# Another order for the seven block products of an MLP down-projection, and its b12 loads issued from GpSimd

## The chip, the cores and the metric

The kernel runs on one core of a Trainium2 chip. The metric is device microseconds of one execution; before the change the median of three runs is 2301.19 us (2300.75 to 2302.45). Engines are named as the profile names them: PE (TensorE), DVE (VectorE), ACT (ScalarE), POOL (GpSimd), SP (SyncE, which here only issues DMAs).

## The reference, cut to what matters

Two layers over 256 tokens of width 2048, each a mixer (HGRN2, then gated linear attention) and an MLP, every sub-layer between two RMSNorms and added to the residual. The change lies in the MLP:

```python
def sqrelu_mlp(h, w_up, w_down):
    u = jax.nn.relu(h @ w_up)        # 256 x 2048 by 2048 x 8192
    return (u * u) @ w_down          # 256 x 8192 by 8192 x 2048
...
f = sqrelu_mlp(rmsnorm(h, norm_mlp_pre[i]), mlp_w_up[i], mlp_w_down[i])
h = h + rmsnorm(f, norm_mlp_post[i])
```

All is float32. The kernel multiplies in fp32r with each operand split in a rounded high part and the rest (hi and lo), and adds three products: hi by hi, hi by lo, lo by hi.

## The kernel before, in words

**Splitting.** Weights arrive as "raw" tiles of 128 x 2048 (1 MB) from SP's queue (line 107, three buffers). Each half of a tile is split: ACT writes hi (line 113, `split_hi`), DVE writes lo = raw - hi (line 117, `split_lo`). There are five buffers of hi halves and five of lo halves.

**Groups.** The hidden width of 8192 is worked in eight groups g of 1024. `up(g)` makes the group's activations in eight up products (`gemmT`, lines 165 and 168: 16 matmuls of 512 columns and 16 of 256), and after each pair it combines them into `as` tiles (lines 534 to 542): differences of activations between the two token halves and the two halves of the group, named R, S, S5 and S3.

**Seven products.** The down-projection of a group uses the trick of seven block products in place of eight, on a two by two scheme: two token halves t, two halves h of the group, and a pair of column blocks n0, n1 (512 columns each). Write b11, b21 for the weight blocks of h = 0 and 1 with n0, b12, b22 with n1. The generator `seven(g, p, following)` gives one product at each step (12 matmuls, line 643, split in two halves). Its tiles:

- `run` (pool `sum`, one buffer): first b11 + b12, summed on DVE (line 655); then b22 is added, then b21, each by one accumulating DMA of 1 MB from POOL (`add_to`, line 601).
- `q` (tiles accA and accB, one buffer each): b12, loaded by `load_b12` (line 608) for the following iterator once the present one has split its own q; b22 is added to it by two accumulating DMAs of 512 KB.

The products before, in order: b11 product (bank a), c product (b21, bank c), **first run product** (S by `run`, bank b), S3 product (b22, bank b), **second run product** (S5 by `run`, bank a), q product (R by q, bank a), **third run product** (pure activations by `run`, bank a). The accumulating DMA between two run products can be issued only when both halves of `run` are split for the one, and the splitting for the other can start only when it has landed.

**Full groups.** With p = 0 the columns n0, n1 are blocks 0 and 1, with p = 1 blocks 2 and 3. Groups 1, 3 and 5 (`both`) use `seven` twice; they are the three full groups, in each of the two MLPs. The other groups do blocks 2 and 3 by plain products (`plain`, lines 145 to 147).

**Order.** The loop over g makes group g's eight up products, and between them does steps of group g - 1 by the table `plan`: entry k of it is done after the k-th up product. `a` and `b` are steps of the two iterators, `late` the last step of a full group's second iterator, which falls in the next group's loop. Tile's scheduler then orders each engine's instructions by its own estimate of the time; each engine runs its list strictly in order. So a PE matmul that waits holds all that is behind it.

Of the kernel before, what the change touches and what calls it, by code (L numbers as in the profile page):

```python
# [30 lines left out]
def trunk(  # L31
# [5 lines left out]
    nc = tc.nc  # L37
# [36 lines left out]
    def nm(s):  # L74
        uid[0] += 1
        return f"{s}_{uid[0]}"
# [26 lines left out]
    def load_chunk(wap, idx):  # L103
        if idx in ahead and ahead[idx][0] is wap:
            return ahead.pop(idx)[1]
        raw = wraw.tile([P, 2, 1024], F32, tag="raw", name=nm("raw"))
        nc.sync.dma_start(raw, wap[idx].rearrange("p (k n) -> p k n", k=2))
        return raw
# [10 lines left out]
    def split(raw, into=None):  # L119

        half = split_hi(raw, into)
        split_lo(raw, half)
        return half
# [382 lines left out]
    def mlp(layer, w_up, w_dn, X, rs, ps0, then=None):  # L506
# [22 lines left out]
        R, S, S5, S3 = range(4)  # L529
# [51 lines left out]
        def up(g):  # L581

            for i in range(HK):
                u = tok().rearrange("p (a n) -> p a n", a=2)
                unfold(gemmT(w_up, g * GK + i, X), u[:, 0, :])
                yield
                if i == 0:
                    uT[g] = Xhl(GK)
                    sa[g] = sums_of_a(g)
                unfold(gemmT(w_up, g * GK + HK + i, X), u[:, 1, :])  # L590
                relu_squared(g, u, [i, HK + i])
                yield
                b = u.rearrange("p a (t n) -> p (a t) n", t=NT)
                combine(sa[g][i], b[:, 0, :], b[:, 2, :], b[:, 1, :], b[:, 3, :], b[:, 1:3, :])

        def block(g, h, n):

            return w_dn[n * 16 + 2 * g + h].rearrange("p (k n) -> p k n", k=2)

        def add_to(raw, b):  # L600
            nc.gpsimd.dma_start(raw, b, accum_op=ALU.add)  # L601

        b12 = []

        def load_b12(g, p):
            b12.append([accp.tile([P, 1024], F32, tag=tag, name=nm("bs")) for tag in ("accA", "accB")])
            for j in range(2):
                nc.sync.dma_start(b12[-1][j], block(g, 0, 2 * p + 1)[:, j, :])

        def put(n, t, ps, sign=1):  # L610
            if (n, t) not in m:
                m[n, t] = tok()
                V.tensor_scalar(m[n, t], ps, float(sign), None, ALU.mult)
            else:
                V.tensor_tensor(m[n, t], m[n, t], ps, ALU.add if sign > 0 else ALU.subtract)

        def seven(g, p, following):


            U, n0, n1 = uT[g], 2 * p, 2 * p + 1  # L620
            bank = {}

            def pure(t, h):
                return lambda k: U(HK * h + k, t)

            def summed(c):
                return lambda k: (sa[g][k][:, 0, c, :], sa[g][k][:, 1, c, :])

            def raw_of(h, n):
                raw = load_chunk(w_dn, n * 16 + 2 * g + h)  # L630
                return [raw[:, j, :] for j in range(2)]

            def product(b, x, raw, n, t, sign=1):
                first = b not in bank
                if first:
                    pool, tag = (pstr, "tr") if b == "c" else (pssc, "sc")
                    bank[b] = pool.tile([P, NB], F32, tag=tag, name=nm(f"s{b}"))
                for j in range(2):
                    hi, lo = (w.rearrange("p (k n) -> p k n", k=2) for w in split(raw[j]))
                    for kk in range(2):  # L640
                        xh, xl = x(2 * j + kk)
                        for i, (l, r) in enumerate(((xh, hi), (xh, lo), (xl, hi))):
                            PE.matmul(bank[b], l, r[:, kk, :], start=first and j + kk + i == 0,  # L643
                                      stop=j + kk + i == 4, skip_group_check=not first)
                put(n, t, bank[b], sign)

            b11 = raw_of(0, n0)
            product("a", pure(1, 0), b11, n0, 1)
            yield
            product("c", pure(1, 1), raw_of(1, n0), n0, 1)  # L650
            yield
            tile_ = sump.tile([P, 2, 1024], F32, tag="run", name=nm("bs"))
            run, q = [tile_[:, j, :] for j in range(2)], b12.pop(0)
            for j in range(2):
                V.tensor_tensor(run[j], b11[j], q[j], ALU.add)
            for j in range(2):
                add_to(q[j], block(g, 1, n1)[:, j, :])
            product("b", summed(S), run, n1, 0, -1)
            add_to(tile_, block(g, 1, n1))
            yield  # L660
            product("b", summed(S3), raw_of(1, n1), n1, 1, -1)
            yield
            product("a", summed(S5), run, n1, 1, -1)
            add_to(tile_, block(g, 1, n0))
            yield
            product("a", summed(R), q, n1, 0, -1)
            if following is not None:
                load_b12(*following)
            yield
            product("a", pure(0, 1), run, n0, 0)  # L670
            yield
# [3 lines left out]
        def plain(g, n):  # L675

            ps = [psmm.tile([P, NB], F32, tag="mm", name=nm("mm")) for _ in range(NT)]
            for c in range(2):
                for j, half in enumerate(split_chunk(w_dn, n * 16 + 2 * g + c)):
                    for t in range(NT):  # L680
                        mm_half(ps[t], half, 2 * c + j, uT[g], t, GK)
                if c:
                    for t in range(NT):
                        put(n, t, ps[t])
                yield
# [6 lines left out]
        for i, (g, p) in enumerate(order):  # L692
            it[g, p] = seven(g, p, order[i + 1] if i + 1 < len(order) else None)

        def step(*what):

            for w in what:
                next(w)
# [3 lines left out]
        first = up_first()  # L702
        next(first)
        load_b12(0, 0)
        for _ in first:
            pass
        for g in range(1, NG):
            u = up(g)
            a = it[g - 1, 0]
            late = [it[g - 2, 1]] if g - 2 in both else []  # L710
            n2, n3 = (plain(g - 1, n) for n in (2, 3))
            if g - 1 in both:
                b = it[g - 1, 1]
                plan = [[*late, a, a], [a, a], [a], [a], [a, b, b], [b, b], [b], [b]]
            elif g < LAST:
                plan = [[*late, a, a], [a, n2], [a, n2], [a], [n3, a], [n3], [a], []]
            else:
                plan = [[*late, a, a], [a], [a], [a], [a], [a], [], []]
            for what in plan:
                next(u)  # L720
                step(*what)
            next(u, None)
        new_residue()
        nc.sync.dma_start(residue[-1], spill)
        a = it[LAST, 0]
        step(n2, a, a, a, n2, a, n3, a, n3, a)
        g = LAST
        n2 = plain(g, 2)
        for t, n in ((0, 1), (1, 0), (1, 1)):
            post.take(m[n, t], n, t)  # L730
        if ahead is not None:
            ahead.split(2)
# [350 lines left out]

    st = hgrn((2, w_up0, 0, ((w_up0, 4, 2), (w_up0, 5, 1))))
    st = mlp(0, w_up0, w_dn0, *st, then=(1, w_gin, 16, ((w_gr, 0, 2), (w_gin, 20, 1))))
    st = gla(*st, then=(3, w_up1, 0, ((w_up1, 4, 2), (w_up1, 5, 1))))
    mlp(1, w_up1, w_dn1, *st)


# [70 lines left out]
```

## Time and profile before

| | |
|---|---|
| median of three runs | 2301.19 us |
| the profiled execution | 2299.35 us, its span 2297.5 us |
| PE busy | 98% of the span |
| DVE, ACT busy | 78%, 59% |
| POOL, accumulating loads (line 601) | 88, median 8.5 us to landing |
| SP, b12 loads (line 608) | 44 of 512 KB, median 7.6 us to landing |
| HBM | 222 GB/s over the span |

In the profile a group of instructions is named by line, engine, operation and out<-in; buffer numbers are left out. The up products write `mmT`, the block products `sa`, `sb`, `sc` (banks a, b, c); `sa<-hi,as` is a product with combined activations, `sa<-hi,xhl` one with pure ones. The tiles `run` and `q` both have the name `bs`. A wait in square brackets is idle time of the engine just before that instruction, with what ended it. PE's matmuls overlap in the records; the distance of their starts is what one costs. The granted clock is that of PE, 1.00 at full speed.

### The profile page before, as it was taken

To read this page: it belongs to the slowest core of one execution; us is meant where nothing else is said; L and a number is where in the kernel's file an instruction comes from. 1 tells how busy PE (TensorE), PEld (TensorE's weight loads), DVE (VectorE), ACT (ScalarE), POOL (GpSimd) and SP (SyncE) were. 2 spreads that over 40 slices of the span, in tenths; PEclk is the share of its full clock that TensorE was granted. 3 is DMA by queue.
4 is the path that set the end of the run, shared out by engine and by line. 5 is a ranking of instruction groups with operands and counts; after the bars stand their busy time and mean duration, and the time that the engine had idled before them with its cause. 6 is when DMAs were issued, how large, how long until landed. Compare 5 with 4: busy or idle time off the path is not lost.

```text
span 2297.5 us, 30042 instructions
## 1 busy us (share of the span) xinstructions
PE 2258.2 (98%) x11456; PEld 1919.0 (84%) x11456; DVE 1797.2 (78%) x2505; ACT 1357.4 (59%) x1843; POOL 76.5 (3%) x92
## 2 busy tenths in 40 slices
PE   9999999999999999999999999999999999999998
PEld 7888888888887887887878887888888788888887
DVE  6887877667788788788886767666778878878887
ACT  7554554556565565566667457555656556556564
POOL 0000000000000000000000000000000000000000
PEclk9999999999999999999999999999999999999999
DMA  9544545557788788778964544455778878878895
GB/s 325 170 165 163 184 151 183 189 214 237 235 254 261 227 248 267 218 244 272 284 237 142 207 157 156 165 206 183 248 232 243 271 237 242 272 231 246 273 290 173
DMA packets 82576, 511.23 MB, mean 223 GB/s; under 512 B 9824, under 2 KB 10208, under 8 KB 28800
## 3 DMA queue, kind: packets, MB, share of 16 engines
q1 hardware_dynamic: 69616, 439.84, 52.0%
q0 software_dynamic: 12672, 69.21, 16.5%
q8 instruction: 90, 1.47, 0.2%
q14 instruction: 54, 0.44, 0.1%
q10 hardware_dynamic: 144, 0.26, 0.0%
HBM read 502.99 MB, written 6.29 MB: 222 GB/s over the span
## 4 chain that ended last, share of the span: by engine, by line
PE 86%; DVE 6%; DMA 5%; issue 1%; ACT 1%; SPq 0%; DVEq 0%; ACTq 0%; POOLq 0%
PE mmT L165 23%; PE mmT L168 13%; PE mm L145 11%; PE mm L147 11%; PE mm L146 11%; PE sa L643 8%; PE sb L643 4%; DMA bs<-w_dn 4%; DVE lo L117 3%; PE sc L643 2%; PE sc L804 2%; DMA raw<-w_dn 1%; PE tr L201 1%; DVE xhl L214 1%; ACT hi L113 1%
## 5 line engine op out<-in xcount | busy, mean ns | idle before, releaser
L117 DVE TENSOR_TENSOR lo<-raw,hi 128x1024 fp32r<-128x1024 f32 x732 | 883.6, 1221 | 264.9 <-ACT hi L113 168.6
L113 ACT ACTIVATE hi<-raw 128x1024 fp32r<-128x1024 f32 x732 | 769.2, 1059 | 511.7 <-PE mm L147 203.2
L165 PE MATMUL mmT<-xhl,hi 128*128 128x512 f32 x2704 | 656.2, 391 | 0.0
L165 PEld LDWEIGHTS mmT<-xhl,hi 128*128 128x128 f32 x2704 | 502.3, 188 | 102.1 <-issue 1.4
L146 PE MATMUL mm<-lo,xhl 128*128 128x512 f32 (+1 forms) x1088 | 423.8, 390 | 2.6 <-DVE lo L283 1.2
L145 PE MATMUL mm<-hi,xhl 128*128 128x512 f32 (+1 forms) x1088 | 421.4, 391 | 1.8 <-ACT hi L282 1.2
L147 PE MATMUL mm<-hi,xhl 128*128 128x512 f32 (+1 forms) x1088 | 422.7, 389 | 0.0
L168 PEld LDWEIGHTS mmT<-xhl,lo 128*128 128x128 f32 x2704 | 351.6, 191 | 15.2 <-issue 0.5
L168 PE MATMUL mmT<-xhl,lo 128*128 128x256 f32 x2704 | 358.3, 283 | 0.0
L113 ACT ACTIVATE hi<-bs 128x1024 fp32r<-128x1024 f32 x176 | 185.1, 1059 | 168.0 <-DMA bs<-w_dn 92.1
L117 DVE TENSOR_TENSOR lo<-bs,hi 128x1024 fp32r<-128x1024 f32 x176 | 213.3, 1221 | 80.1 <-ACT hi L113 77.7
L146 PEld LDWEIGHTS mm<-lo,xhl 128*128 128x128 f32 x1088 | 204.5, 188 | 45.1 <-DVE lo L283 2.7
L145 PEld LDWEIGHTS mm<-hi,xhl 128*128 128x128 f32 x1088 | 204.5, 188 | 44.4 <-ACT hi L282 2.8
L147 PEld LDWEIGHTS mm<-hi,xhl 128*128 128x128 f32 x1088 | 204.4, 188 | 42.0 <-issue 0.6
L601 POOL DMA_DIRECT2D bs<-w_dn x88 | 76.3, 875 | 2174.6 <-DVE lo L117 574.1
L643 PE MATMUL sa<-hi,as 128*128 128x512 f32 x352 | 117.5, 395 | 22.2 <-ACT hi L113 22.2
L643 PE MATMUL sb<-hi,as 128*128 128x512 f32 x352 | 121.2, 406 | 0.0
L643 PE MATMUL sa<-hi,xhl 128*128 128x512 f32 x352 | 114.3, 390 | 0.0
L643 PEld LDWEIGHTS sa<-hi,as 128*128 128x128 f32 x352 | 66.4, 189 | 36.3 <-ACT hi L113 23.8
L643 PEld LDWEIGHTS sb<-hi,as 128*128 128x128 f32 x352 | 69.9, 198 | 14.3
L643 PEld LDWEIGHTS sa<-hi,xhl 128*128 128x128 f32 x352 | 66.2, 188 | 13.2
L643 PE MATMUL sb<-lo,as 128*128 128x512 f32 x176 | 71.7, 407 | 0.0
(210 smaller groups left out, 2013.8 us busy)
## 6 DMA issues: line engine op xcount, KB each, us to landing
raw<-w_up SPq DMA_DIRECT2D x128, 1024.0 KB, 6.7
raw<-w_dn SPq DMA_DIRECT2D x106, 1024.0 KB, 7.0
raw<-w_hin SPq DMA_DIRECT2D x56, 1024.0 KB, 4.9
raw<-w_gin SPq DMA_DIRECT2D x48, 1024.0 KB, 4.9
bs<-w_dn POOLq DMA_DIRECT2D x44, 1024.0 KB, 8.8
bs<-w_dn SPq DMA_DIRECT2D x44, 512.0 KB, 7.6
bs<-w_dn POOLq DMA_DIRECT2D x44, 512.0 KB, 7.3
raw<-w_hout SPq DMA_DIRECT2D x16, 1024.0 KB, 4.9
```

Source lines behind the costliest of these rows:

```text
L113: A.activation(hi, raw, AF.Copy)
L117: V.tensor_tensor(half[1], raw, half[0].bitcast(F32), ALU.subtract)
L145: PE.matmul(ps, xh, hi[:, kk, cs], start=(k == 0), stop=False)
L146: PE.matmul(ps, xh, lo[:, kk, cs], start=False, stop=False)
L147: PE.matmul(ps, xl, hi[:, kk, cs], start=False, stop=(k == nk - 1))
L165: PE.matmul(ps, hi, X.both(k), start=(k == 0), stop=False)
L168: PE.matmul(ps[:, 0, :], lo, X.both(k)[:, 0, :], start=False, stop=(k == KT - 1))
L201: PE.transpose(ps[:, j, :], src(j), ident)
L214: V.scalar_tensor_tensor(lo[:, j, :], ps[:, j, :], gain(j), hi[:, j, :].bitcast(F32), ALU.mult, ALU.subtract)
L601: nc.gpsimd.dma_start(raw, b, accum_op=ALU.add)
L643: PE.matmul(bank[b], l, r[:, kk, :], start=first and j + kk + i == 0, stop=j + kk + i == 4, skip_group_check=not first)
L804: PE.matmul(ps[:, hd, :], l(hd * kt + k), r(hd * kt + k), start=(k == 0), stop=(k == kt - 1))
```

## The change

In `seven` the first run product goes to the front, the b11 and c products follow it, and the second run product comes ahead of the S3 product: first run, b11, c, second run, S3, q, third run. `plan` shares the steps out evenly: in a full group two at a time after the up products 1, 2, 3, then one, then two at a time for the second iterator; entry 0 holds only `late`. The plans of the other groups and the steps after the last group follow. The b12 loads go from SP's queue to POOL's. The order in which three finished blocks are normed at the end of an MLP is swapped for two of them.

```diff
         def load_b12(g, p):
             b12.append([accp.tile([P, 1024], F32, tag=tag, name=nm("bs")) for tag in ("accA", "accB")])
             for j in range(2):
-                nc.sync.dma_start(b12[-1][j], block(g, 0, 2 * p + 1)[:, j, :])
+                nc.gpsimd.dma_start(b12[-1][j], block(g, 0, 2 * p + 1)[:, j, :])
...
             b11 = raw_of(0, n0)
-            product("a", pure(1, 0), b11, n0, 1)
-            yield
-            product("c", pure(1, 1), raw_of(1, n0), n0, 1)
-            yield
             tile_ = sump.tile([P, 2, 1024], F32, tag="run", name=nm("bs"))
...
             product("b", summed(S), run, n1, 0, -1)
             add_to(tile_, block(g, 1, n1))
             yield
-            product("b", summed(S3), raw_of(1, n1), n1, 1, -1)
+            product("a", pure(1, 0), b11, n0, 1)
+            yield
+            product("c", pure(1, 1), raw_of(1, n0), n0, 1)
             yield
             product("a", summed(S5), run, n1, 1, -1)
             add_to(tile_, block(g, 1, n0))
+            yield
+            product("b", summed(S3), raw_of(1, n1), n1, 1, -1)
             yield
             product("a", summed(R), q, n1, 0, -1)
...
             if g - 1 in both:
                 b = it[g - 1, 1]
-                plan = [[*late, a, a], [a, a], [a], [a], [a, b, b], [b, b], [b], [b]]
+                plan = [late, [a, a], [a, a], [a, a], [a], [b, b], [b, b], [b, b]]
             elif g < LAST:
-                plan = [[*late, a, a], [a, n2], [a, n2], [a], [n3, a], [n3], [a], []]
+                plan = [late, [a, a], [a, n2], [n2, a], [a, a], [a, n3], [n3], []]
             else:
-                plan = [[*late, a, a], [a], [a], [a], [a], [a], [], []]
+                plan = [late, [a, a], [a], [a], [a], [a], [a], []]
...
-        step(n2, a, a, a, n2, a, n3, a, n3, a)
+        step(n2, a, a, n2, a, n3, a, n3, a, a)
...
-        for t, n in ((0, 1), (1, 0), (1, 1)):
+        for n, t in ((0, 1), (1, 0), (1, 1)):
             post.take(m[n, t], n, t)
```

The scheduler's lists show it at three places. First ACT in the second iterator of group 1 of the first MLP, from the second half of the first run product to the first half of the second one (`bs_1052` and `bs_1041` are the `run` tile). Before:

```order
L113 ACTIVATE hi_1056_6126<-bs_1052_6110 128x1024
L541 ACTIVATE as_787_4635<-tok_1020_5938 128x512
L113 ACTIVATE hi_1059_6140<-raw_1058_6138 128x1024
L113 ACTIVATE hi_1061_6150<-raw_1058_6138 128x1024
L113 ACTIVATE hi_1067_6171<-raw_1066_6169 128x1024
L557 COPY half_1051_6103<-mmT_1045_6060 128x256
L113 ACTIVATE hi_1069_6175<-raw_1066_6169 128x1024
L113 ACTIVATE hi_1072_6214<-bs_1052_6110 128x1024
```

And with the change:

```order
L113 ACTIVATE hi_1045_6080<-bs_1041_6064 128x1024
L113 ACTIVATE hi_1048_6093<-raw_1040_6062 128x1024
L541 ACTIVATE as_787_4635<-tok_1020_5938 128x512
L113 ACTIVATE hi_1050_6103<-raw_1040_6062 128x1024
L113 ACTIVATE hi_1056_6124<-raw_1055_6122 128x1024
L557 COPY half_1039_6055<-mmT_1033_6012 128x256
L113 ACTIVATE hi_1058_6128<-raw_1055_6122 128x1024
L113 ACTIVATE hi_1063_6170<-raw_1061_6167 128x1024
L113 ACTIVATE hi_1065_6180<-raw_1061_6167 128x1024
L551 ACTIVATE xhl_963_5638<-tok_1021_5944 128x2x256
L552 ACTIVATE tok_1021_5944<-tok_1021_5944 128x512
L113 ACTIVATE hi_1067_6191<-bs_1041_6064 128x1024
```

Between the two run products stood the halves of the S3 product and of one up product; now the halves of the b11 product, of one up product and of the c product stand there.

Second, DVE where `run` is summed for that iterator (line 655 before, 651 with the change). Before:

```order
L655 TENSOR_TENSOR bs_1052_6110<-raw_1033_6012,bs_1018_5934 128x1024
L655 TENSOR_TENSOR bs_1052_6110<-raw_1033_6012,bs_1019_5935 128x1024
L553 TENSOR_TENSOR xhl_975_5686<-tok_995_5794,xhl_975_5686 128x2x256
L534 TENSOR_TENSOR tok_1020_5938<-tok_995_5794 128x256
L117 TENSOR_TENSOR lo_1038_6026<-raw_1033_6012,hi_1037_6025 128x1024
```

With the change:

```order
L651 TENSOR_TENSOR bs_1041_6064<-raw_1040_6062,bs_1018_5934 128x1024
L117 TENSOR_TENSOR lo_1036_6016<-raw_1034_6013,hi_1035_6015 128x1024
L651 TENSOR_TENSOR bs_1041_6064<-raw_1040_6062,bs_1019_5935 128x1024
L539 SCALAR_TENSOR_TENSOR tok_1020_5938<-tok_1020_5938,tok_984_5747 128x128
L117 TENSOR_TENSOR lo_1038_6020<-raw_1034_6013,hi_1037_6019 128x1024
L117 TENSOR_TENSOR lo_1044_6071<-bs_1041_6064,hi_1043_6070 128x1024
```

Before, the splits of the b11 product, of the c product and of an up product lay between the sums and the split of `run`; now the split of `run` follows behind the split of one up product.

Third, POOL from the adds into one `run` tile to those into the next, with the change:

```order
L601 DMA bs_972_5691<-w_dn0 128x2048 x2
L608 DMA bs_1018_5934<-w_dn0 128x1024
L608 DMA bs_1019_5935<-w_dn0 128x1024
L601 DMA bs_1018_5934<-w_dn0 128x1024
L601 DMA bs_1019_5935<-w_dn0 128x1024
L601 DMA bs_1041_6064<-w_dn0 128x2048 x2
```

The two rows of line 608 stood in SP's list before, among the raw loads; POOL's list was the same without them.

## The prediction

> **What bounds the kernel now.** I read the page first: the busy shares (part 1) and the chain of waits (part 4).
>
> ```profile
> PE 2258.2 (98%) x11456; PEld 1919.0 (84%) x11456; DVE 1797.2 (78%) x2505; ACT 1357.4 (59%) x1843; POOL 76.5 (3%) x92
> ...
> PE 86%; DVE 6%; DMA 5%; issue 1%; ACT 1%; SPq 0%; DVEq 0%; ACTq 0%; POOLq 0%
> ```
>
> TensorE sets the time, and there is little to win off it: what PE itself loses is the budget. The table of waits says where it loses.
>
> ```profile
> PE sa L643 <- ACT hi L113: 22.2, 7, 4.5
> ...
> ACT hi L113 <- DMA bs<-w_dn: 92.1, 23, 7.8
> ...
> ACT hi L113 <- DMA raw<-w_dn: 61.1, 29, 3.5
> ...
> SPq L608 <- DVE lo L117: 52.5, 32, 2.8
> ```
>
> PE has one large wait: 22.2 us in seven pieces before a block product that goes to bank "a". It waits there for the rounding of a `bs` tile on ScalarE, and ScalarE waits for the DMA into that tile. Raw weight loads also hold ScalarE (61.1 us), but no row of PE names them: the work queued ahead covers them. Next, the timeline at the first of the long pieces (DVE, POOL, ACT and PE, each asked for by itself).
>
> ```profile
> 683.89 2.35 DVE L117 TENSOR_TENSOR lo<-bs,hi 128x1024 fp32r<-128x1024 f32 x2
> ```
> ```profile
> 675.96 0.86 POOL L601 DMA_DIRECT2D bs<-w_dn  x1 [0.27 <-issue]
> 686.54 0.86 POOL L601 DMA_DIRECT2D bs<-w_dn  x1 [9.72 <-DVE lo L117]
> ```
> ```profile
> 698.59 2.00 ACT L113 ACTIVATE hi<-bs 128x1024 fp32r<-128x1024 f32 x2 [6.77 <-DMA bs<-w_dn]
> ```
> ```profile
> 688.75 0.40 PE L643 MATMUL sb<-hi,as 128*128 128x512 f32 x1
> ...
> 691.50 3.79 PE L165 MATMUL mmT<-xhl,hi 128*128 128x512 f32 x16
> 695.13 1.11 PE L168 MATMUL mmT<-xhl,lo 128*128 128x256 f32 x8
> 699.70 0.50 PE L643 MATMUL sa<-hi,as 128*128 128x512 f32 x1 [3.46 <-ACT hi L113]
> ```
>
> This is the second iterator (p = 1) of a full group. DVE ends the split of `run` for the first run product at 686.2; GpSimd then issues the accumulating DMA into `run` (686.54); its data is there at 698.59, 12.05 us later; ScalarE rounds it in 1.1 us; PE starts the second run product at 699.70. PE had reached that matmul at about 696.1 (695.13 and eight 256-wide matmuls): the room for the DMA was 696.1 - 1.1 - 686.54 = 8.5 us. Last the windows, one for each full group's loop, and one loop without a full group.
>
> ```profile
> 630.80:716.40 85.60, 82.14 (x416) 70.11 (x416) 71.12 (x89) 52.46 (x63) 5.17 (x6) 0.98 0.81 247
> 716.40:804.20 87.80, 87.80 (x449) 75.21 (x448) 72.99 (x90) 51.06 (x59) 5.17 (x6) 1.00 0.80 249
> 804.20:891.10 86.90, 82.93 (x415) 70.50 (x414) 71.75 (x91) 52.57 (x64) 5.17 (x6) 0.96 0.81 249
> 978.90:1065.70 86.80, 82.34 (x416) 70.25 (x415) 71.42 (x90) 52.54 (x63) 5.20 (x6) 0.98 0.80 245
> 1730.00:1813.70 83.70, 80.41 (x416) 68.86 (x415) 69.47 (x87) 50.48 (x61) 5.17 (x6) 1.00 0.81 248
> 1901.80:1987.80 86.00, 82.02 (x415) 70.00 (x415) 70.51 (x89) 52.19 (x63) 5.17 (x6) 0.98 0.81 247
> 2075.60:2160.70 85.10, 82.04 (x416) 70.02 (x415) 71.52 (x90) 52.70 (x63) 5.20 (x6) 0.98 0.82 251
> ```
>
> The columns are the stretch, its length, busy time of PE, weight loads, DVE, ACT and POOL, the granted clock, the DMA share and GB/s. All six loops of a full group lose time, the other loop none. They also lose clock: times the lengths, the shares missing from 1.00 are 1.7 + 3.5 + 1.7 + 0 + 1.7 + 1.7 = 10.3 us. What a loop should take comes from these rows of PE:
>
> ```profile
> 589.54 0.40 PE L643 MATMUL sa<-hi,as 128*128 128x512 f32 x1
> ...
> 592.29 3.79 PE L165 MATMUL mmT<-xhl,hi 128*128 128x512 f32 x16
> 595.91 2.08 PE L168 MATMUL mmT<-xhl,lo 128*128 128x256 f32 x16
> 597.83 0.40 PE L145 MATMUL mm<-hi,xhl 128*128 128x512 f32 x1
> ```
>
> A block product takes 592.29 - 589.54 = 2.75 us, an up product 597.83 - 592.29 = 5.54. A full loop has 8 up and 13 block products: 44.3 + 35.8 = 80.1 us. The six loops last 514.1 us against 480.4: 33.7 us too long, which 22.2 (wait) + 10.3 (clock) = **32.5 us** explains to 1.2 us.
>
> **The change, part by part.** Instruction counts and arithmetic stay; PE's work is the same. *First: the run products move apart.* In the full groups' second iterator, the ones that wait now, the first run product is now followed by the b11 product, an up product and the c product before the second: start to start 2.75 + 2.75 + 5.54 + 2.75 = 13.8 us, where before PE came to it after 696.1 - 688.75 = 7.3. The DMA was issued 2.2 us before the first run product started; with that lead the room becomes 13.8 + 2.2 - 1.1 = 14.9 us, with a lead of 1 us (the sum is now formed right ahead of its split) 13.7. Landings:
>
> ```profile
> DMA to landing us min/median/max: 5.5/8.5/11.9
> ```
> ```profile
> DMA to landing us min/median/max: 4.4/7.6/9.3
> ```
> ```profile
> bs<-w_dn SPq DMA_DIRECT2D x44, 512.0 KB, 7.6
> bs<-w_dn POOLq DMA_DIRECT2D x44, 512.0 KB, 7.3
> ```
>
> The first line is of L601, the accumulating loads; the second of L608, the b12 loads. 13.7 is above the longest, 11.9, so the wait goes: -22.2. One thing speaks for a remainder: the two adds into `q` are now issued some 5 us ahead of this one instead of 686.54 - 675.96 = 10.6, and of their 7.3 us about 2.3 are then still to move. 11.9 + 2.3 = 14.2 against 13.7: between 0 and 0.5 us in each of six loops, 0 to 3.0; I take 1.5.
>
> *The clock.* Without the long waits I take all 10.3 us back, since the loop without a wait has 1.00. How long a wait may be without costing clock the rows leave uncertain:
>
> ```profile
> 1798.64 0.50 PE L643 MATMUL sa<-hi,as 128*128 128x512 f32 x1 [3.29 <-ACT hi L113]
> ```
> ```profile
> 2144.03 0.50 PE L643 MATMUL sa<-hi,as 128*128 128x512 f32 x1 [3.06 <-ACT hi L113]
> ```
>
> 3.29 us cost nothing (its loop has 1.00), 3.06 cost 1.7. [...]
>
> *The third run product.* Second to third run product was 16.6 us in the waiting iterator (run, up, q, up, as the plan has it); it is now run, S3, q, up = 13.8. The same 13.7 to 14.9 against 11.9: 0.
>
> *The b12 loads on GpSimd's queue.* They are freed by the split of `q` and are needed by the sum of the next iterator, now its first step. From q product to that first run product lie q, up, third run product, up = 16.6 us of PE. The load is issued about as the q product starts; 11.9 us is the longest landing on that queue; the sum and one rounding follow:
>
> ```profile
> L655 DVE TENSOR_TENSOR bs<-raw,bs 128x1024 f32<-128x1024 f32 x44 | 51.8, 1220 | 11.7 <-DMA raw<-w_dn 11.7
> ```
>
> 11.9 + 2 x 1.22 + 1.06 (as 2.00 for two above) = 15.4 in 16.6: hidden, by 1.2 us at worst. If that cover were gone, 2.4 us at a start. On GpSimd nothing urgent stands behind the load: the next DMA is the add into the same tile. SP loses the 52.5 us it stood at L608; as PE never waits for raw loads, 0. [...]
>
> *The first run product needs the group's combined activations at once.* Before, two pure products covered them. From the copy of an up product's result to the end of the combination:
>
> ```profile
> 589.74 0.37 ACT L557 COPY half<-mmT 128x256 f32<-128x256 f32 x1 [0.85 <-PE mmT L168]
> ```
> ```profile
> 599.40 0.68 DVE L542 TENSOR_TENSOR as<-tok,as 128x512 fp32r<-128x512 f32 x1
> ```
>
> 10.5 us after the up product ended. Cover now: two up products (11.1), and nine matmuls until the last quarter is used (2.0), 13.1: hidden, 2.6 us spare. If it were not, up to 10.5 - 5.5 = 5 us in each of 16 groups.
>
> Sum: -22.2 - 10.3 + 1.5 = -31.0 on the profiled span: 2297.5 - 31.0 = 2266.5. That execution lasted 2299.35 us, 1.85 more than its span and 1.84 below the median of the runs: 2301.19 - 31.0 = **2270 us**.
>
> **The rivals.** (1) *The DMA stays late, less so.* The full loops already have a DMA share of 0.81; without the waits the same bytes go into 80 us, 0.81 x 85.6 / 80.1 = 0.87. If that stretches landings by a quarter (11.9 to 14.9) and the q adds add 2.3, PE waits 17.2 - 14.9 to 17.2 - 13.7, some 2.3 to 3.5 us: at 2.3, without clock loss, 13.8 us over six loops, 2301.2 - 32.5 + 13.8 = 2282. For it: the 12.05 us landing fell in such a crowd. Against: b11 is now held shorter, and fewer loads crowd around it.
> (2) *The change doesn't do what it says.* The scheduler set PE's order, and had put the second run product ahead of the S3 product in the loop above; if it hoists it again, or the same wait turns up at the third, nothing is won: 2299 to 2303. Against: the built order has the c product ahead of it.
> (3) *Slower: DVE at the start of each iterator.* Up, first run and b11 product are 11.0 us of PE. Of DVE's 71 us in a full loop, 42 splits of 1.14 (2.35 for two at 683.89) are 47.9 and four sums 4.9; the rest, 18.2, is 0.87 for each of the 21 products. Here that makes six splits 6.8, two sums 2.4 and three times 0.87, 11.8 us. The five buffers for split halves are a lead (a half feeds 1.4 us of PE in a block product, 2.8 in an up product), in which 0.8 us should drown. If DVE has no lead there, the sums are paid in full at all 22 starts: 51.8 us (the row of L655), 2301.2 - 32.5 + 51.8 = 2320; it decides from 1.5 us a start (32.5 / 22). For it: DVE is 71 us busy in a full loop that is to take 80. Against: in the present trace the sums stand in the same stream, and PE shows no wait on DVE there.
>
> **How the numbers follow.** A measurement of this kernel tells 0.2%, 4.6 us, from no change. Chances: forecast 0.66 (2265 to 2277), (1) 0.19 (2277 to 2293), (2) 0.05, (3) 0.10. Faster 0.85, same 0.05, slower 0.10. The floor is all 33.7 us and a little, 2265; the range reaches through most of (1): 2264 to 2289.
>
> **What would show it.** In the changed profile the PE row on bank "a" waiting for ScalarE should be gone or below 3 us in sum; full loops should last 80 to 81 us at 1.00; DMA share there 0.85 or more. Wrong if a new PE wait on DVE's `lo` or on `hi<-bs` appears at a first run product, if the sum (now L651) shows waits for `bs` loads, or if the half-clock stretches stay without waits.

## The result, and the profile after

The changed kernel takes 2266.78 us, the median of four runs (2266.16 to 2267.66). The kernel before takes 2301.82 us in the same comparison (four runs, 2300.75 to 2303.19). The ratio is 0.9848, with a 95% interval of 0.9831 to 0.9865: the change makes the kernel 1.5% faster. The profiled execution lasted 2267.66 us, its span 2265.9 us.

First the page of the changed kernel, the busy shares and the chain of waits by engine:

```profile
PE 2247.6 (99%) x11456; PEld 1913.6 (84%) x11456; DVE 1798.9 (79%) x2505; ACT 1365.5 (60%) x1843; POOL 101.1 (4%) x136
...
PE 94%; DVE 3%; DMA 1%; ACT 1%; issue 0%; SPq 0%; DVEq 0%; ACTq 0%
```

PE's share of the chain went from 86% to 94%, and DVE's and DMA's shrank from 6% and 5% to 3% and 1%. POOL's 44 more instructions are the b12 loads. The tables of waits of the changed kernel, PE's longest row and then ScalarE's rows on transfers in the MLP (us in total, times, longest):

```profile
PE tr L201 <- DVE h L354: 3.3, 5, 0.9
```
```profile
ACT hi L113 <- DMA raw<-w_dn: 17.7, 9, 3.5
ACT hi L113 <- DMA bs<-w_dn: 11.9, 6, 2.8
ACT hi L113 <- DMA raw<-w_up: 11.4, 9, 2.9
```

The row of 22.2 us on bank a is gone; PE's longest row now has nothing to do with the block products. ScalarE waited 92.1 us for `bs` tiles before, 11.9 us now, and 61.1 and 17.7 us for raw down weights. Landings of the accumulating loads (line 601), where the longest was 11.9:

```profile
DMA to landing us min/median/max: 5.5/8.5/12.5
```

They are much as before. Now the windows of the six full loops, each from the first up product of the group behind a full group to that of the next group (13 block products in each):

```profile
630.80:711.10 80.30, 80.30 (x416) 69.02 (x416) 72.41 (x91) 53.51 (x64) 7.39 (x10) 1.00 0.92 273
798.90:879.20 80.30, 80.30 (x416) 69.01 (x416) 72.16 (x91) 53.16 (x64) 7.41 (x10) 1.00 0.90 268
966.80:1047.20 80.40, 80.40 (x417) 69.11 (x416) 72.56 (x91) 53.41 (x64) 7.39 (x10) 1.00 0.93 273
1710.30:1790.70 80.40, 80.40 (x417) 69.11 (x416) 72.38 (x91) 53.41 (x64) 7.39 (x10) 1.00 0.92 273
1878.30:1958.70 80.40, 80.40 (x418) 69.08 (x417) 72.26 (x91) 53.22 (x64) 7.38 (x10) 1.00 0.92 273
2046.20:2126.60 80.40, 80.40 (x417) 69.10 (x416) 72.26 (x91) 53.16 (x64) 7.38 (x10) 1.00 0.90 266
```

PE is busy over the whole length of each, at full clock. The six last 482.2 us together, where they lasted 514.1 us: 31.9 us less, as much as the span lost (2297.5 - 2265.9 = 31.6). So the whole gain is in the full groups. The transfers are denser than before: the share of the DMA engines is 0.90 to 0.93 where it was 0.80 to 0.82.

The same place as in the prediction, the second iterator of the first full group, in the timeline (POOL, ACT and PE in turn):

```profile
673.88 0.89 POOL L601 DMA_DIRECT2D bs<-w_dn  x1 [8.38 <-DVE bs L651]
676.14 0.88 POOL L601 DMA_DIRECT2D bs<-w_dn  x1 [1.38 <-DVE tok L539]
680.28 0.86 POOL L601 DMA_DIRECT2D bs<-w_dn  x1 [3.26 <-DVE lo L117]
```
```profile
691.40 2.01 ACT L113 ACTIVATE hi<-bs 128x1024 fp32r<-128x1024 f32 x2 [1.42 <-DMA bs<-w_dn]
```
```profile
683.42 0.40 PE L643 MATMUL sb<-hi,as 128*128 128x512 f32 x1
...
697.18 0.39 PE L643 MATMUL sa<-hi,as 128*128 128x512 f32 x1
```

The first two rows are the adds into `q`, the third is the add into `run`, issued 3.1 us before the first run product starts. ScalarE gets its data 11.1 us later. PE comes to the second run product at 697.18 and finds the first half rounded since 692.5: 4.7 us to spare, where it was 3.5 us short.

### The profile page after: what moved, and what is told of

Same layout as the page of the kernel before. It is cut to its first block, busy times and chain, and to the rows that moved or that the text cites. A ratio compares the mean times of both kernels' runs of the same rounds, so it can differ in the third digit from the quotient of the medians.

```text
span 2265.9 us, 30032 instructions
## 1 busy us (share of the span) xinstructions
PE 2247.6 (99%) x11456; PEld 1913.6 (84%) x11456; DVE 1798.9 (79%) x2505; ACT 1365.5 (60%) x1843; POOL 101.1 (4%) x136
## 4 chain that ended last, share of the span: by engine, by line
PE 94%; DVE 3%; DMA 1%; ACT 1%; issue 0%; SPq 0%; DVEq 0%; ACTq 0%
PE mmT L165 27%; PE mmT L168 14%; PE mm L145 10%; PE mm L146 10%; PE mm L147 10%; PE sa L643 10%; PE sb L643 5%; PE sc L643 3%; PE sc L804 2%; DMA wp<-npost 1%; DVE lo L117 1%; DVE xhl L214 1%; PE tr L201 1%; DVE h L354 0%; PE sd L839 0%
## 5 line engine op out<-in xcount | busy, mean ns | idle before, releaser
L168 PE MATMUL mmT<-xhl,lo 128*128 128x256 f32 x2704 | 353.5, 283 | 0.0
L601 POOL DMA_DIRECT2D bs<-w_dn x88 | 76.6, 871 | 926.1 <-DVE lo L117 391.3
L557 ACT COPY half<-mmT 128x256 f32<-128x256 f32 x120 | 44.4, 370 | 72.0 <-PE mmT L168 71.8
L643 PEld LDWEIGHTS sa<-hi,xhl 128*128 128x128 f32 x352 | 66.2, 188 | 13.4
L608 POOL DMA_DIRECT2D bs<-w_dn x44 | 24.3, 553 | 1187.5 <-PE mm L147 974.4
```

The source lines that it names most:

```text
L168: PE.matmul(ps[:, 0, :], lo, X.both(k)[:, 0, :], start=False, stop=(k == KT - 1))
L557: A.copy(x, ps[:, 1, :])
L608: nc.gpsimd.dma_start(b12[-1][j], block(g, 0, 2 * p + 1)[:, j, :])
```

## The experiments

**The theory** to be tested: PE lost time because the accumulating DMA into `run` landed later than PE came to the next run product. What ends the wait is the distance between the run products in the order inside `seven`; the clock comes back with the wait; the new `plan` and GpSimd's queue carry nothing of the gain. **The rivals**: the gain comes from the queue (the b12 loads no longer stand in SP's list); it comes from the evener `plan`; or the order is near a limit on DVE that a little more work at an iterator's start would show. Ratios are to the kernel before, with 95% intervals.

| run | median us | ratio |
|---|---|---|
| change | 2266.78 | 0.9848 (0.9831 to 0.9865) |
| order only | 2267.53 | 0.9856 (0.9841 to 0.9870) |
| GpSimd's queue only | 2300.41 | 0.9999 (0.9987 to 1.0010) |
| order and queue, old plan | 2266.96 | 0.9848 (0.9834 to 0.9863) |
| new plan, old order | 2328.30 | 1.0124 (1.0109 to 1.0139) |
| before, first add in halves | 2279.44 | 0.9908 (0.9892 to 0.9925) |
| change, first add twice | 2403.30 | 1.0441 (1.0425 to 1.0456) |
| change, four split buffers | 2269.33 | 0.9856 (0.9840 to 0.9873) |
| change, sums twice | 2314.09 | 1.0049 (1.0032 to 1.0066) |
| the same and halves | 2324.34 | 1.0100 (1.0083 to 1.0116) |
| change, DVE work behind | 2268.31 | 0.9857 (0.9841 to 0.9874) |
| sums twice, q adds behind | 2350.55 | 1.0206 (1.0185 to 1.0228) |
| the same, short reader | 2337.41 | 1.0144 (1.0115 to 1.0173) |

### Which part of the change carries the gain

*Order only*: the changed kernel with the b12 loads back on SP's queue.

```diff
-                nc.gpsimd.dma_start(b12[-1][j], block(g, 0, 2 * p + 1)[:, j, :])
+                nc.sync.dma_start(b12[-1][j], block(g, 0, 2 * p + 1)[:, j, :])
```

> The new order and plan, with the b12 loads issued from SP as before. Theory (the wait is the landing of the accumulating DMA, about 12 us, against the room between two run products, 8.5 us before and 13.7 to 14.9 now): the room is the same as in the changed kernel, so 2265 to 2270 us and no PE wait on bank a above 1 us in sum. Rival Q (the gain comes from the b12 loads leaving SP's queue, where raw loads stood behind them): the waits come back at least in part, 2280 to 2300 us.

It took 2267.53 us, and PE has no wait on bank a. *GpSimd's queue only*: the kernel before with its one line turned the other way.

> The order and plan of before, with the b12 loads issued from GpSimd. Theory: the room stays 8.5 us, the PE row on bank a stays at 20 to 25 us, the half-clock stretches stay; 2297 to 2306 us. Rival Q: most of the gain is here, 2267 to 2285 us.

2300.41 us, the kernel before within its interval. Its table of waits keeps the old row:

```profile
PE sa L643 <- ACT hi L113: 20.4, 7, 3.9
```

The queue by itself does nothing. *Order and queue, old plan*: the changed kernel with the three `plan` lines of the kernel before; the line for a full group is shown.

```diff
-                plan = [late, [a, a], [a, a], [a, a], [a], [b, b], [b, b], [b, b]]
+                plan = [[*late, a, a], [a, a], [a], [a], [a, b, b], [b, b], [b], [b]]
```

> The new order of the seven products under the old plan of steps; b12 loads from GpSimd. In a full group the second iterator's first run product now comes right behind the first iterator's third one, with no up product between. Theory: the room from first to second run product is still above 12 us, so that wait is gone; the sum into run (2.4 us of DVE) and one rounding (1.1) can start only when the third run product is split, so PE waits 0 to 3 us at six places: 2266 to 2286 us. Rival P (the plan of steps carries the gain): 2295 us or more.

2266.96 us, as the change. *New plan, old order*: the kernel before with the three `plan` lines of the changed one; the same line is shown.

```diff
-                plan = [[*late, a, a], [a, a], [a], [a], [a, b, b], [b, b], [b], [b]]
+                plan = [late, [a, a], [a, a], [a, a], [a], [b, b], [b, b], [b, b]]
```

> The old order of the seven products under the new plan of steps (two at a time after the up products 1, 2, 3 and 5, 6, 7 of a full group); b12 loads from SP. Theory: between the first and second run product still stand the S3 product and one up product, so the room stays 8.5 us and the waits stay, now perhaps in both iterators of a full group: 20 to 45 us of PE wait on bank a, 2298 to 2335 us. Rival P (the even spread of the steps is what helps): 2266 to 2280 us.

2328.3 us, slower than before by 1.2%. Its waits of PE before up and block products, and ScalarE's waits for transfers:

```profile
PE mmT L165 <- ACT hi L113: 29.3, 20, 3.2
PE mmT L168 <- DVE lo L117: 10.3, 11, 1.1
PE sa L643 <- ACT hi L113: 5.5, 5, 3.4
```
```profile
ACT hi L113 <- DMA bs<-w_dn: 121.3, 33, 7.3
ACT hi L113 <- DMA raw<-w_up: 63.6, 15, 6.5
```

The time is within what was expected, but not the place: 20 to 45 us of wait were expected on bank a, and 5.5 were measured, so the time fits by luck. The two run products are no closer than before: 7.3 to 7.5 us from start to start in a full group without the waits, 7.3 to 7.8 there. PE's wait shows mostly on up products (29.3 and 10.3 us): a half of an up product stands in ScalarE's list behind a half of `run` whose data has not come, or waits for its own late load. Of the 17 waits of the first row that last over 0.9 us, ScalarE had last waited for a raw up load in 11 (20.7 us together) and for a `bs` tile in 6 (7.3 us). So most of this row goes back to late up weights (63.6 us of ScalarE's waits against 7.9 before); why the even plan delays them stays open. The order in `seven` carries the whole gain: with it the plan is indifferent, and without it the even plan costs 1.2%.

### Is it the landing against the room

The trace of the kernel before has a first answer. In the first iterator of the same full group the two run products also start 7.3 us apart, and PE doesn't wait (POOL, ACT and PE):

```profile
644.29 0.86 POOL L601 DMA_DIRECT2D bs<-w_dn  x1 [22.60 <-DVE lo L117]
```
```profile
652.68 1.06 ACT L113 ACTIVATE hi<-bs 128x1024 fp32r<-128x1024 f32 x1 [2.61 <-DMA bs<-w_dn]
```
```profile
647.42 0.40 PE L643 MATMUL sb<-hi,as 128*128 128x512 f32 x1
...
654.75 0.40 PE L643 MATMUL sa<-hi,as 128*128 128x512 f32 x1
```

Its data is there 8.4 us after the issue, where the second iterator's takes 12.05. In all six full groups the distance without the waits is about the same in both iterators (7.3 to 7.8 us); the landing is 8.2 to 8.8 us in the first ones, where PE waits once, for 0.4 us, and 11.0 to 11.9 us in the second ones, where it waits 3.1 to 4.5 us each time. So the distance alone does not make the wait; the landing against it does. Why data lands later in the second iterator stays open.

*Before, first add in halves*: the kernel before, with the first add into `run` cut in two of 512 KB, each issued when its own half is split. The order stays.

```diff
-            add_to(tile_, block(g, 1, n1))
+            for j in range(2):
+                add_to(run[j], block(g, 1, n1)[:, j, :])
```

> The kernel before, with the first accumulating DMA into run cut into two of 512 KB, each issued behind the split of its own half. The order of the products is the old one. Theory: the room stays, but the first half is issued 1.1 us earlier and lands after 7 to 9 us in place of 12, the second half is wanted 1.4 us later; the wait falls from 3.1 to 4.5 us to 0 to 1.5 us in each full group, and with it the clock loss: 2268 to 2281 us. Rival 1 (the transfer engines are crowded, so that two halves land no earlier than one whole): the wait stays above 2.5 us, 2290 to 2302 us.

2279.44 us, 22.4 us less than before, as expected. The row of 22.2 us is gone; the largest before a block product are now:

```profile
PE sa L643 <- DVE tok L615: 2.9, 6, 0.6
PE sa L643 <- DVE lo L117: 2.3, 7, 0.4
```

At the known place ScalarE has the first half 8.3 us after its issue (692.35 - 684.04), and PE starts the second run product 7.3 us after the first, without a wait. So with the old order too the wait goes when the first half of the data comes earlier. 12.7 us above the change remain, of which these rows carry 5.2. *Change, first add twice*: the changed kernel, with the first add into `run` issued twice in a row (`run` then holds b22 twice).

```diff
             add_to(tile_, block(g, 1, n1))
+            add_to(tile_, block(g, 1, n1))
```

> The changed kernel with the first accumulating DMA into run issued twice (b22 is added twice, so the result of the products with S5 and of the third run product is another one; 22 MB more traffic). The second lands only after the first: some 17 to 22 us from the first issue. Theory: against a room of 13.7 to 14.9 us PE waits 3 to 7 us in the second iterator of each full group, 18 to 42 us, and loses 1.7 to 3.4 us of clock at each: 2290 to 2325 us. If landing does not decide, the time stays at 2267 to 2272 us.

2403.3 us, beyond the range expected: the direction was right, the size not, for the expectation counted one iterator of each full group and both of them wait. PE's row:

```profile
PE sa L643 <- ACT hi L113: 82.7, 16, 7.5
```

At the place shown above the second add was issued only when the first had landed, 11.6 us after it:

```profile
687.79 0.86 POOL L601 DMA_DIRECT2D bs<-w_dn  x1 [3.27 <-DVE lo L117]
699.43 0.85 POOL L601 DMA_DIRECT2D bs<-w_dn  x1 [10.78 <-DMA bs<-w_dn]
```

With two landings in the room of one, the wait on bank a comes back, in 16 places instead of seven, and with it the loss of clock (0.976 over the span, where the change has 0.998; by these two an estimated 0.022 x 2400 = 53 us). These two runs show the mechanism from both sides: less landing removes the wait in the old order, more landing brings it back in the new one.

### How near the new order is to a limit on DVE

*Change, four split buffers*: one buffer less for hi halves and for lo halves.

```diff
-    wsp = ctx.enter_context(tc.tile_pool(name="wsp", bufs=5))
+    wsp = ctx.enter_context(tc.tile_pool(name="wsp", bufs=4))
```

> The changed kernel with four buffers for hi halves and four for lo halves in place of five. Everything else is the same. It takes one half (1.4 us of PE in a block product, 2.8 in an up product) from the lead of ACT and DVE. Theory with a lead of several us: PE begins to wait on splits at the crowded places, the time grows by 5 to 60 us: 2272 to 2327 us. If the time stays within 2 us, the lead is never used, and rival 3 is further off than thought.

2269.33 us, below what was expected, 2.6 us above the change, and by the intervals not to be told from it: the fifth buffer is hardly used. *Change, sums twice*: both sums that form `run` are computed twice, 2.3 us more of DVE work at each start.

```diff
-                V.tensor_tensor(run[j], b11[j], q[j], ALU.add)
+                for _ in range(2):
+                    V.tensor_tensor(run[j], b11[j], q[j], ALU.add)
```

> The changed kernel with each sum b11 + b12 into run computed twice on DVE (the same values, 2.4 us more of DVE at each of the 22 starts). Theory: DVE's lead over PE drowns it, 2266 to 2271 us. Rival 3 (DVE has no lead at the start of an iterator, so that the sums are paid on PE's path): 22 x 2.4 = 52 us more in part or in full, 2285 to 2319 us.

2314.09 us: missed by far. 44 more instructions of 1.2 us, 54 us on an engine that has time, cost 47 us. PE's row, and at the known place POOL, ACT and PE:

```profile
PE mmT L165 <- ACT hi L113: 26.9, 12, 3.2
```
```profile
683.52 0.86 POOL L601 DMA_DIRECT2D bs<-w_dn  x1 [2.19 <-DVE lo L117]
```
```profile
696.95 2.00 ACT L113 ACTIVATE hi<-bs 128x1024 fp32r<-128x1024 f32 x2 [6.66 <-DMA bs<-w_dn]
...
699.38 1.04 ACT L113 ACTIVATE hi<-raw 128x1024 fp32r<-128x1024 f32 x1
```
```profile
683.80 0.40 PE L643 MATMUL sb<-hi,as 128*128 128x512 f32 x1
...
700.47 1.65 PE L165 MATMUL mmT<-xhl,hi 128*128 128x512 f32 x3 [2.75 <-ACT hi L113]
```

The sums stand ahead of the split of `run`, so the add was issued 0.3 us before the first run product instead of 3.1, and its data came 13.4 us later instead of 11.1. By the distance of the changed kernel's run products (697.18 - 683.42 = 13.8) PE is due at the second one at 697.6; the first half is rounded by 698.0, 0.4 us late. PE waits 2.75 us, because the next up product, whose first matmuls PE's list has ahead of the second run product, needs a half that ScalarE rounds only at 699.38, behind both halves of `run` and another activation. So data that is 0.4 us late for its own product is 2.75 us late for what stands behind it. From this first run product to the next one, of the following group, it is 45.8 us here and 41.3 in the changed kernel; the wait and the slower matmuls behind it (nine take 3.58 us from 700.47 to 704.05, where nine at the 0.23 us of the rows around them take 2.07, so an estimated 1.5 us lost) are 4.3 of these 4.5 us. Six of the row's twelve waits are of this kind, one in each full group (2.5 to 3.2 us, 16.7 together). The other six (10.2 us) fall in the loop behind; there ScalarE has waited not for `run` but, in at least five of them, for a raw load. That is a reading of one trace; the next runs tell it from a plain shortage on DVE.

*Change, DVE work behind*: as many DVE instructions of the same shape, but behind the splits of the b11 product.

```diff
             product("a", pure(1, 0), b11, n0, 1)
+            for j in range(2):
+                V.tensor_tensor(b11[j], b11[j], b11[j], ALU.add)
             yield
```

> The changed kernel with two more DVE instructions of 128x1024 at each start, as many as the doubled sums brought, but placed behind the splits of the b11 product (they add the spent b11 tile to itself, which nothing reads), so behind the issue of the first add into run. Theory 'lead': the add is issued as early as in the changed kernel, so nothing is lost: 2266 to 2272 us. Theory 'DVE': the same 2.3 us of work in each start cost as much as ahead of the add: 2295 to 2317 us.

2268.31 us: 1.5 us instead of 47. The add into `run` goes out as early as in the changed kernel, 3.1 us before the first run product:

```profile
679.82 0.86 POOL L601 DMA_DIRECT2D bs<-w_dn  x1 [3.26 <-DVE lo L117]
```
```profile
682.96 0.40 PE L643 MATMUL sb<-hi,as 128*128 128x512 f32 x1
```

PE's list has matmuls of an up product ahead of the second run product here too (four, from 696.72), so that order alone costs nothing either. It is not that DVE has no time at a start; what counts is whether the work stands ahead of the split that releases the add. *Sums twice and halves*: the run with doubled sums, with the first add cut in halves as above.

> The changed kernel with each sum of run formed twice, as in the run that came out at 2314.09 us, but the first add into run cut in two DMAs of 512 KB, each issued behind the split of its own half. Theory 'lead': the doubled sums cost time only because the split of run, and with it the first add, comes 2.3 us later, so that its landing exceeds the room; a first half that leaves 1 to 2 us earlier and is smaller brings the lead back: 2266 to 2285 us, PE's row on up products behind ScalarE under 8 us. Theory 'DVE': 2.3 us more work on DVE at a start are too much for it as such: 2305 to 2317 us, with PE waits on DVE's lo or on half-full lists, whatever the DMAs do.

2324.34 us, slower still, above what either theory had. The two halves were issued at 681.82 and 682.96, but ScalarE waited for each of them:

```profile
681.82 0.86 POOL L601 DMA_DIRECT2D bs<-w_dn  x1 [1.07 <-DVE lo L117]
682.96 0.85 POOL L601 DMA_DIRECT2D bs<-w_dn  x1 [0.28 <-DVE lo L117]
```
```profile
693.66 1.06 ACT L113 ACTIVATE hi<-bs 128x1024 fp32r<-128x1024 f32 x1 [3.93 <-DMA bs<-w_dn]
698.63 1.06 ACT L113 ACTIVATE hi<-bs 128x1024 fp32r<-128x1024 f32 x1 [3.91 <-DMA bs<-w_dn]
```

The first half took 11.8 us and the second 15.7, though each moves half the bytes of the 1 MB add that took 11.1. Cutting the add helped in the old order and hurts here, where the two adds into `q` leave 4.5 and 1.9 us ahead of it; that these are the reason is what the next two runs look into.

*Sums twice, q adds behind*: the adds into `q` are put behind the first add into `run`, held back by an addition that reads `q`.

```diff
-            for j in range(2):
-                add_to(q[j], block(g, 1, n1)[:, j, :])
             product("b", summed(S), run, n1, 0, -1)
             add_to(tile_, block(g, 1, n1))
             yield
             product("a", pure(1, 0), b11, n0, 1)
+            for j in range(2):
+                V.tensor_tensor(b11[j], b11[j], q[j], ALU.add)
+                add_to(q[j], block(g, 1, n1)[:, j, :])
             yield
```

> The changed kernel with each sum formed twice (2314.09 us by itself), and the two adds into q moved from ahead of the first add into run to behind it: each is issued when DVE has added q to the spent b11 tile (an addition that nothing reads; work of this kind at this place cost nothing in the run that had it alone). In the run with doubled sums the add into run was issued 0.2 us ahead of the first run product and landed 13.3 us later, with the two adds into q issued 5.7 and 3.1 us ahead of it. Theory 'crowd': the landing is that long because the adds into q are still moving; alone it lands within 9 to 10 us, and the time goes back to 2266 to 2275 us, PE's wait on up products behind ScalarE below 5 us. Theory 'issue': what counts is only that the add is issued 2.3 us later, whatever moves beside it: 2300 to 2317 us, with the row of about 27 us on PE still there.

2350.55 us, slower than either theory had. At the known place the add into `run` is there 8.2 us after its issue (694.91 - 686.72), as 'crowd' had it, but ScalarE waits 120.2 us for raw weights in the MLPs (63.0 for up and 57.2 for down weights). *The same, short reader*: the added additions take 128 columns only.

> As the run with doubled sums and the adds into q behind the first add into run (2350.55 us), but what holds the adds into q back is an addition of 128 columns instead of 1024 on each half of the spent b11 tile, so that DVE has some 2.2 us less to do at a start and the b11 tile is given back to the raw loads earlier. Theory 'crowd': the add into run lands 8 to 10 us after its issue as in that run, the raw loads come earlier than there, and the time falls below that of the doubled sums alone: 2266 to 2290 us, PE's waits on hi of up products under 12 us. Theory 'moved queue': in this stretch the transfer engines have no room, so the adds into q behind delay the raw loads instead of the add into run, and PE waits for these: 2300 to 2345 us, with ScalarE waiting for raw loads 60 us or more.

2337.41 us, in the range of the theory of the moved queue. Its add into `run`, and what ScalarE waits for, at the known place and in all:

```profile
683.31 0.89 POOL L601 DMA_DIRECT2D bs<-w_dn  x1 [18.15 <-DVE lo L117]
```
```profile
691.45 2.01 ACT L113 ACTIVATE hi<-bs 128x1024 fp32r<-128x1024 f32 x2 [3.00 <-DMA bs<-w_dn]
698.41 1.06 ACT L113 ACTIVATE hi<-raw 128x1024 fp32r<-128x1024 f32 x1 [3.77 <-DMA raw<-w_up]
```
```profile
ACT hi L113 <- DMA raw<-w_up: 79.5, 28, 5.4
ACT hi L113 <- DMA raw<-w_dn: 52.6, 24, 5.8
```

Issued ahead of the adds into `q`, the add into `run` is there after 8.1 us. But now ScalarE waits 132.1 us for raw weights, where the changed kernel has 17.7 + 11.4 = 29.1. Two things delay the raw loads. They land later: the longest landing (line 107) went from 11.8 us in the changed kernel to 18.4. And they are issued later, since SP has to wait for the added additions, which read the b11 tile and so hold its buffer:

```profile
SPq L107 <- DVE raw L658: 220.2, 22, 12.2
```

The up load for which ScalarE waits until 698.41 was issued at 687.82; in the changed kernel it was issued at 683.99. So the adds do crowd one another, but that the raw loads pay for it in transfer time alone is not shown: the edit also holds their buffer. What stays open is how much lead a start can lose before PE waits: less than the 2.3 us tried. No variant beat the change; PE is busy 99% of its span.

## Why the prediction was right

Forecast 2270 us, measured 2266.78, within the range and by the mechanism named.

**The wait on bank a, -22.2**: right. The room came out a little larger than assumed: the add left 3.1 us before the first run product, not 1 to 2.2, so the room is 697.18 - 1.1 - 680.28 = 15.8 us against the top of 14.9. The longest landing on line 601 went to 12.5 us, but here it is 11.1.

**The adds close ahead, +1.5**: this term was mis-sized; it is 0. They were feared to push the landing to 14.2 us. They left 6.4 and 4.1 us ahead of the add into `run`, one further ahead than the 5 us assumed, and the landing here is shorter than before (12.05). The runs with doubled sums show that the mechanism itself exists, only on the other side of the edge: with the adds 5.7 and 3.1 us ahead it is 13.4 us, and with none ahead (the short reader) 8.1.

**The clock, -10.3**: right, all six windows show 1.00. The size was read in one execution, and it differs between executions of the kernel before: thirteen of them, run beside the first experiments, take 2298.11 to 2306.58 us with a clock of 0.995 to 0.992. No wait was left that would have tried how long one may be without costing clock.

**The covers taken at nothing** (third run product, b12 loads, combined activations): right, none of them shows in PE's waits. The sum (line 651) never had DVE idle before it, where in the kernel before it waited 11.7 us for raw loads; b12 on SP or on GpSimd is 0.75 us apart, inside the spread of the runs.

**The loop**: 80.1 us was worked out from single rows, 80.3 to 80.4 were measured. **The sum**: -31.0 forecast, -31.6 on the span. That they agree so well is partly luck, as the second is the difference of two single executions: the medians lie 2301.82 - 2266.78 = 35.0 us apart, 4.0 more than the sum. The time was missed by 3.4 us (2301.19 - 31.0 = 2270.19); 0.6 of it is the sum on the span. The rest is the last step, the way from the span to the median: 1.85 us beside the span and 1.84 for a profiled execution below its median. The first is 1.76 in the changed kernel; the second turned round, its profiled execution is 0.88 above the median. Which way one execution falls can't be foreseen.

**The rivals.** (1) *The DMA stays late*: its premise was right, its inference wrong. It expected the DMA share to rise to 0.87; it rose to 0.90 to 0.93, yet landings on line 601 did not stretch by a quarter (longest 11.9 before, 12.5 now). (2) fell with the row of PE, and the order came out as the change says. (3) *DVE at the start* did not come about, but the reason given against it was weak. The five split buffers were said to be a lead in which 0.8 us drown; four do as well. What carries the start is the time between the issue of the add and the first run product, and 2.3 us of DVE work ahead of it cost 47 us, while behind it they cost 1.5. The rival's price of 51.8 us was near those 47, but by a mechanism that it did not have: twelve waits behind late data, not 22 sums paid in full (at the known place the first run product starts at 683.80 us with the doubled sums and at 683.42 without). In that rival's working half of 2.35 us was taken as 1.14, where it is 1.18; its 11.8 us become 11.9, and nothing hangs on it.

## What to carry to other kernels

Where a buffer is refilled by DMA between two uses, compare the landing with the distance of the uses on the bounding engine, and reorder independent work into that distance before touching queues: here that is the whole 1.5%. Then look at what stands ahead of the instruction that releases the DMA: the same work on the same engine, 79% busy, cost 47 us there and 1.5 us a few instructions later. And look at what is next in the list of an engine that waits: with the doubled sums, data 0.4 us late for its own product cost PE a wait of 2.75 us before another.

## What was not expected of the hardware

**The length of a wait did not decide the clock.** In the run of the kernel before with the first add in halves, PE's wait at 872 us is 1.25 us long, and half clock follows (columns as in the windows above):

```profile
872.39 0.98 PE L165 MATMUL mmT<-xhl,hi 128*128 128x512 f32 x3 [1.25 <-ACT hi L113]
```
```profile
874.10:877.50 3.40, 3.40 (x10) 2.62 (x9) 3.40 (x5) 2.47 (x5) 0.86 (x1) 0.50 0.58 80
```

In the run with doubled sums a wait of 3.23 us is followed by full clock:

```profile
2152.38 0.96 PE L165 MATMUL mmT<-xhl,hi 128*128 128x512 f32 x3 [3.23 <-ACT hi L113]
```
```profile
2150.50:2154.00 3.50, 1.62 (x7) 1.37 (x8) 2.92 (x5) 3.50 (x7) 0.85 (x1) 1.00 0.43 183
2154.00:2157.50 3.50, 3.50 (x18) 2.88 (x17) 3.50 (x6) 3.28 (x5) 0.00 (x0) 1.00 0.94 147
```

So whether a wait cost clock was not decided by its length alone.

When the half clock sets in says more. In the trace of the kernel before, apart from the kernel's two ends, it begins at 701.20, 871.87, 1049.36, 1970.96 and 2145.04 us and lasts 3.41 us each time, the second time 6.82; the distances between these starts are 170.67, 177.49, 921.60 and 174.08 us, which is 50, 52, 270 and 51 times 3.4133 (1443.84 / 423). Three of the waits in stretches of this length, counted from these starts (length, then PE's busy time; the clock is the third column from the end):

```profile
697.79:701.20 3.41, 1.50 (x8) 1.31 (x9) 1.22 (x1) 2.57 (x4) 0.00 (x0) 1.00 0.80 336
701.20:704.61 3.41, 3.41 (x10) 2.64 (x9) 2.79 (x5) 2.48 (x3) 0.10 (x1) 0.50 0.02 7
...
1793.47:1796.88 3.41, 1.89 (x13) 1.53 (x11) 0.00 (x0) 0.00 (x0) 0.00 (x0) 1.00 0.99 308
1796.88:1800.29 3.41, 1.65 (x9) 1.44 (x10) 1.23 (x1) 2.72 (x4) 0.00 (x0) 1.00 0.92 389
1800.29:1803.71 3.42, 3.42 (x19) 2.93 (x18) 2.95 (x5) 3.28 (x4) 0.26 (x1) 1.00 0.01 5
...
2141.63:2145.04 3.41, 1.01 (x6) 0.92 (x7) 1.03 (x1) 2.12 (x3) 0.00 (x0) 1.00 0.99 418
2145.04:2148.45 3.41, 3.41 (x10) 2.64 (x9) 2.50 (x6) 3.04 (x4) 0.00 (x0) 0.50 0.04 14
```

In this trace the five stretches at full clock in which PE idled for 1.91, 1.97, 2.40, 3.08 and 3.15 us were each followed by half clock, and none with 1.76 us or less was (again without the two ends). The wait of 3.29 us before 1798.64 lay across two of them, with 1.52 and 1.76 us of idle time, and cost nothing; that of 3.06 us before 2144.03 lies with 2.40 us in one, and cost clock. That the idle time of such a stretch decides was not shown: with the first add in halves the two waits of PE ahead of the half clock, 1.25 us before 872.39 and 0.27 before 873.64, make 1.52 us together. Why they cost clock stays open.

**Accumulating loads took twice the transfer time of plain ones.** The page of the kernel before, where all of POOL's DMAs accumulate and none of SP's does (packets, MB, share of 16 engines' span):

```profile
q1 hardware_dynamic: 69616, 439.84, 52.0%
q0 software_dynamic: 12672, 69.21, 16.5%
```

That is 0.12% a MB for the plain loads and 0.24% for the accumulating ones, twice as much. The queue is not the reason. In the run with GpSimd's queue only, the b12 loads, 23.07 MB that don't accumulate, are in the same queue (the page of the changed kernel has the same line):

```profile
q0 software_dynamic: 19008, 92.28, 19.4%
```

They added 2.9%, so 0.13% a MB, as little as on SP's queue. The price of the accumulating ones fits the tightness seen above (a DMA share of 0.90 to 0.93): by 0.24 against 0.12% a MB, two accumulated copies of a block cost the transfer engines what four plain ones would.
